# Eight first-product chunks parked in DRAM, two more ahead of the first second product, and top-k casts on ScalarE

## The chip, the cores and the metric

The kernel runs on one core of a Trainium2 chip. The metric is the device time of one execution in microseconds (us), given as the median of several runs. Beside it there is one profiled execution, from which all rows below come. Engines are named as the profile does: PE (TensorE matmul), PEld (its weight loads), DVE (VectorE), ACT (ScalarE), POOL (GpSimd), SP (SyncE, which issues DMAs).

## What is computed

A residual block over 512 tokens of width 1024: a mixer (chunked attention and a state-space layer), a cross-attention, and an expert layer. Only the expert layer is touched. It has 16384 experts of one neuron each, whose keys are pairs out of 128 × 128; each of 8 heads picks 16 experts for a token.

```python
def _peer_ffn(hn, w_q, sub_keys, u_tab, v_tab):
    ...
    def block(xb):                       # 128 tokens
        q = (xb @ w_q).reshape(PEER_BLOCK, PEER_HEADS, 2, PEER_QDIM // 2)
        s = jnp.einsum('thsd,hsnd->thsn', q, sub_keys).astype(jnp.float32)
        sv, si = lax.top_k(s, PEER_TOPK)
        cand = (sv[:, :, 0, :, None] + sv[:, :, 1, None, :]).reshape(PEER_BLOCK, PEER_HEADS, -1)
        cidx = (si[:, :, 0, :, None] * PEER_KEYS + si[:, :, 1, None, :]).reshape(PEER_BLOCK, PEER_HEADS, -1)
        top, pos = lax.top_k(cand, PEER_TOPK)
        e = jnp.take_along_axis(cidx, pos, axis=-1)
        g = jax.nn.softmax(top, axis=-1)
        act = jax.nn.gelu(jnp.einsum('thkd,td->thk', u_tab[e], xb), approximate=False)
        w = (g * act).astype(xb.dtype)
        return jnp.einsum('thk,thkd->td', w, v_tab[e])
```

## The kernel before

The 512 tokens are four blocks of 128. Three of them (384 tokens) are computed densely: all 16384 experts are gone through in 128 chunks of 128, and a table of gates, mostly zeros, picks the chosen ones. The fourth block is gathered: 128 rows of the first table and 128 of the second are fetched for each token by indirect DMAs on POOL's queue, and DVE multiplies and adds them.

The work on the path has four stages.

1. *Top-k* (about 500 to 660 us in the trace). For each head h, `queries(h)` makes the queries and scores on PE, and ACT copies them out of PSUM (`pqT`, `sc`, `scl`). `topk(h, scs, g)` then works for the token blocks of group g (blocks 0 and 1, block 2, block 3): DVE finds the 16 best of each half (`tv`, `ti`), casts their places to float (`tf`), DVE adds the candidates (`ca`) and POOL their numbers (`cx`), DVE finds the 16 best candidates and their places (`pi`, cast to `pf`). A one-hot of the places (`eq`, DVE) times the numbers (`ev`, POOL), summed by DVE (`ex`), gives the experts' numbers. Beside it run 12 chunks of the first product (`FREE`), their splits on POOL.
2. *Gate table* (`build_w`, about 664 to 818 us). 96 half steps: DVE builds one-hots (`oAE`, `oB`), PE multiplies them (eight matmuls `pw` for a half step), ACT copies the results out (two evictions `stg`), and `Wd` in DRAM takes them. 16 chunks of the first product are spread over these half steps (`LEAD - FREE`), six matmuls at a time.
3. *The loop* `for n in range(128)`. `u_phase(n + 28)` is a chunk of the first product: `load_split` fetches 512 KB of the first table, ACT casts them to the rounded type (`whi`), DVE takes the rest (`wlo`); 24 matmuls of 128x384 go to `pa`, and ACT's Gelu writes an activation tile. `v_phase(n)` is a chunk of the second product: the activation times the table of gates `wt` (DVE), rounded (`ah`, ACT), rest (`al`, DVE), and 18 matmuls of 128x512 into the six accumulators `acc`. The gathers are spread over this loop by a rate (`due`). Block 3's top-k, one head an iteration, runs beside iterations 1 to 8.
4. *The end*: the last 28 iterations hold no first product.

There are 31 activation tiles (`LEAD + 3`). The program text is recorded, and the order of each engine's rows is then set by a list scheduler that simulates the times; `tc.issue_after(x)` ties a row behind the row `x`. DMAs are issued by SP (weights, the table's stores) and ACT (the table's loads). Every engine works through its rows in order.

Of the kernel before, what the change touches and what calls it, by code (L numbers as in the profile page):

```python
# [9 lines left out]
F32 = mybir.dt.float32  # L10
# [5 lines left out]
AF = mybir.ActivationFunctionType  # L16
OP = mybir.AluOpType
AX = mybir.AxisListType
# [783 lines left out]
NT = 384  # L802
LEAD = 28
FREE = 12
HOLD = 10
IOH = 2
ULV = (8,)
KS = 2
H0 = 2
SLACK = 4  # L810
# [5 lines left out]
NC_ = sum(n * w for _, n, w in ROWS)  # L816
# [3 lines left out]
def peer(tc, I, c, out):  # L820
# [5 lines left out]
    with tc.tile_pool(name="pp", bufs=1) as pp, tc.tile_pool(name="tq", bufs=2) as tq:  # L826
# [3 lines left out]
        def act_tile(name):  # L830
            return pp.tile([128, NT], F32, tag="act", name=name, bufs=LEAD + 3)
# [45 lines left out]
        def topk(h, scs, g):  # L877
# [11 lines left out]
            tf = tq.tile([128, 2, nb, 16], F32, tag="tf", name="tf")  # L889
            V.tensor_copy(tf, ti)  # L890
            V.tensor_scalar(tf[:, 0], tf[:, 0], 128.0, None, op0=OP.mult)
            ca = tq.tile([128, nb, NC_], F32, tag="ca", name="ca")
# [12 lines left out]
            for b in range(nb):  # L905
# [5 lines left out]
                V.max_index(pi[:, b, 8:16], tb[:, 8:16], cb)  # L911
            V.tensor_copy(pf, pi)
            for b in range(nb):
                sh = [128, NC_, 16]
                eq = tq.tile(sh, BF16, tag="eq", name="eq")
                ev = pp.tile(sh, F32, tag="ev", name="ev", bufs=1)
                V.tensor_tensor(eq, iob, pf[:, b].unsqueeze(1).broadcast_to(sh), op=OP.is_equal)
                G.tensor_tensor(ev, eq, cx[:, b].unsqueeze(2).broadcast_to(sh), op=OP.mult)
                V.tensor_reduce(ex[:, b0 + b, h], ev.rearrange("p n k -> p k n"), axis=AX.X, op=OP.add)  # L919

# [120 lines left out]

        def u_steps(n):
            w = load_split(I["ut"][n], G if n < FREE else V)
            pa = pst("s", "pa")[:, :NT]
            for k in range(8):
                mm3(pa, [t[:, k] for t in w], [PTh(k)[:, 128:], PTl(k)[:, 128:]], k == 0, k == 7)
                if k < 7 and (k + 1) % KS == 0:
                    yield
            acts[n] = act_tile("act")
            S.activation(acts[n], pa, AF.Gelu)  # L1050
            yield

        def u_phase(n):
            for _ in u_steps(n):
                pass
# [3 lines left out]
        def load_wt(i):  # L1059
            wts[i] = wt = s8([128, 12, 128], "wt")  # L1060
            nc.scalar.dma_start(wt, Wd[i].rearrange("i s c t -> i s (c t)"))

        def v_phase(n):
# [13 lines left out]
            if n % 4 == WTP and n + 4 < 128:  # L1077
                with tc.issue_after(c.ah_ins):
                    load_wt(n // 4 + 1)
            c.v_ins = V.tensor_tensor(al, a, ah, op=OP.subtract).ins  # L1080
            for b in range(3):
# [9 lines left out]
        for n in range(FREE):  # L1091
            u_phase(n)
        steps = (None for n in range(FREE, LEAD) for _ in u_steps(n))
        done = 0
        for q in range(96):
            next(gw)
            if q in LATE:
                i = LATE.index(q)
                with tc.issue_after(c.w_ins):
                    gates(1) if i == H0 else topk_late(8 - H0 + i, 1)  # L1100
            with tc.issue_after(c.pw_ins):
                while done < (q + 1) * (8 // KS) * (LEAD - FREE) // 96:
                    next(steps)
                    done += 1
# [4 lines left out]
        for n in range(128):  # L1109
            if n + LEAD < 128:  # L1110
                u_phase(n + LEAD)
            v_phase(n)
# [10 lines left out]
            if n > HOLD:  # L1123
                due += 256 * (2 if n + LEAD < 128 else 1) / (256 - LEAD - 2 * HOLD - SLACK)
            while due >= 1:
# [80 lines left out]
```

## Time and profile before

| what | value |
|---|---|
| median of three runs | 1779.57 us |
| lowest and highest | 1777.91 and 1783.63 us |
| the profiled execution | 1780.63 us, of which the span 1778.9 us |
| PE busy | 1682.0 us of the span |
| DVE, ACT, POOL busy | 1398.8, 717.6, 689.5 us |

The span is the stretch between the first and the last instruction that the profiler records; 1.7 us lie around it. Busy shares are means over stages with different limits, so they are read by stage below. A matmul's own duration is longer than the step from one to the next, because they overlap: prices of PE's work are taken from starts.

### The profile page before, as it was taken

To read this page: it belongs to the slowest core of one execution; us is meant where nothing else is said; L and a number is where in the kernel's file an instruction comes from. 1 tells how busy PE (TensorE), PEld (TensorE's weight loads), DVE (VectorE), ACT (ScalarE), POOL (GpSimd) and SP (SyncE) were. 2 spreads that over 40 slices of the span, in tenths; PEclk is the share of its full clock that TensorE was granted. 3 is DMA by queue.
4 is the path that set the end of the run, shared out by engine and by line. 5 is a ranking of instruction groups with operands and counts; after the bars stand their busy time and mean duration, and the time that the engine had idled before them with its cause. 6 is when DMAs were issued, how large, how long until landed. Compare 5 with 4: busy or idle time off the path is not lost.

```text
span 1778.9 us, 24797 instructions
## 1 busy us (share of the span) xinstructions
PE 1682.0 (95%) x8929; PEld 1462.1 (82%) x8929; DVE 1398.8 (79%) x2755; ACT 717.6 (40%) x1161; POOL 689.5 (39%) x566
## 2 busy tenths in 40 slices
PE   7898999999999668899999999999999999999999
PEld 6676778877788667788888999999999999999887
DVE  7998563644589999995998787777777877777886
ACT  4242573432333227785333333333333333333332
POOL 5432232341466651200345444444343434334451
PEclk9998999999999889999999999999999999999999
DMA  5412323220422226786449998888888888888895
GB/s 189 115 55 89 113 101 142 95 83 15 175 92 81 66 72 208 213 238 225 163 151 352 331 334 303 308 313 303 306 315 293 331 311 318 297 315 300 324 366 212
DMA packets 155820, 383.19 MB, mean 215 GB/s; under 512 B 13993, under 2 KB 70825, under 8 KB 155569
## 3 DMA queue, kind: packets, MB, share of 16 engines
q1 hardware_dynamic: 107504, 212.83, 35.1%
q0 software_dynamic: 36864, 134.23, 21.1%
q10 hardware_dynamic: 11328, 34.54, 5.5%
q8 instruction: 70, 1.15, 0.2%
q14 instruction: 54, 0.43, 0.1%
HBM read 348.72 MB, written 32.51 MB: 214 GB/s over the span
## 4 chain that ended last, share of the span: by engine, by line
PE 71%; DVE 22%; issue 3%; DMA 2%; POOL 1%; ACT 1%; SPq 0%; DVEq 0%; ACTq 0%; POOLq 0%
PE acc L1084 27%; PE pa L124 8%; PE pa L126 8%; PE pa L125 8%; PE pv L124 3%; PE pv L126 3%; PE pv L125 3%; DVE oB L1023 2%; DVE oAE L1019 2%; DVE ex L919 2%; DVE wlo L110 2%; PE pS L684 1%; PE po L694 1%; DVE ca L898 1%; PE pw L1028 1%
## 5 line engine op out<-in xcount | busy, mean ns | idle before, releaser
L108 ACT ACTIVATE whi<-wraw 128x1024 fp32r<-128x1024 f32 (+1 forms) x332 | 349.7, 1055 | 486.9 <-PE pa L125 229.9
L124 PE MATMUL pa<-PTh,whi 128*128 128x384 f32 x1024 | 355.8, 347 | 21.9 <-ACT act L1050 18.2
L126 PE MATMUL pa<-PTh,wlo 128*128 128x384 f32 x1024 | 350.5, 342 | 14.2 <-POOL wlo L110 10.8
L110 DVE TENSOR_TENSOR wlo<-wraw,whi 128x1024 fp32r<-128x1024 f32 x262 | 321.1, 1226 | 53.4 <-ACT whi L108 53.1
L125 PE MATMUL pa<-PTl,whi 128*128 128x384 f32 x1024 | 349.4, 341 | 0.0
L972 POOL DMA_INDIRECT vg<-in_peer_v_dram,ei x128 | 182.1, 1423 | 240.0 <-DVE X L973 216.7
L962 POOL DMA_INDIRECT ug<-in_peer_u_dram,ei x128 | 177.5, 1386 | 225.2 <-DVE ug L963 201.0
L1084 PE MATMUL acc<-wlo,ah 128*128 128x512 f32 x768 | 238.6, 392 | 0.8 <-DVE wlo L110 0.8
L1084 PE MATMUL acc<-whi,ah 128*128 128x512 f32 x768 | 239.2, 392 | 0.0
L1084 PE MATMUL acc<-whi,al 128*128 128x512 f32 x768 | 237.3, 391 | 0.0
L124 PEld LDWEIGHTS pa<-PTh,whi 128*128 128x128 f32 x1024 | 196.6, 192 | 28.1 <-ACT act L1050 20.3
L110 POOL TENSOR_TENSOR wlo<-wraw,whi 128x1024 fp32r<-128x1024 f32 x70 | 170.2, 2441 | 126.7 <-ACT whi L108 126.6
L126 PEld LDWEIGHTS pa<-PTh,wlo 128*128 128x128 f32 x1024 | 196.8, 192 | 17.2 <-POOL wlo L110 12.4
L125 PEld LDWEIGHTS pa<-PTl,whi 128*128 128x128 f32 x1024 | 196.7, 192 | 3.8
L973 DVE SCALAR_TENSOR_TENSOR X<-vg,dots,X 128x1024 f32<-128x1024 f32 x128 | 164.5, 1285 | 16.3 <-DMA vg<-in_peer_v_dram,ei 10.4
L1076 ACT ACTIVATE ah<-act 128x384 fp32r<-128x384 f32 x128 | 67.1, 526 | 260.7 <-PE acc L1084 241.5
L1084 PEld LDWEIGHTS acc<-wlo,ah 128*128 128x128 f32 x768 | 144.6, 188 | 33.3 <-DVE wlo L110 1.5
L1084 PEld LDWEIGHTS acc<-whi,al 128*128 128x128 f32 x768 | 144.1, 188 | 30.9
L963 DVE SCALAR_TENSOR_TENSOR ug<-ug,X 128x1024 f32<-128x1024 f32 x128 | 151.9, 1222 | 20.6 <-DMA ug<-in_peer_u_dram,ei 20.5
L1084 PEld LDWEIGHTS acc<-whi,ah 128*128 128x128 f32 x768 | 143.2, 188 | 23.7
L1080 DVE TENSOR_TENSOR al<-act,ah 128x384 fp32r<-128x384 f32 x128 | 70.9, 555 | 58.7 <-ACT ah L1076 56.3
L1074 DVE TENSOR_TENSOR act<-act,wt 128x384 f32<-128x384 f32 x128 | 66.0, 576 | 58.3 <-DMA wt<-Wd 58.3
(383 smaller groups left out, 2721.9 us busy)
## 6 DMA issues: line engine op xcount, KB each, us to landing
wraw<-in_ut_dram SPq DMA_DIRECT2D x128, 512.0 KB, 5.0
wraw<-in_peer_v_dram SPq DMA_DIRECT2D x128, 512.0 KB, 5.5
Wd<-stg SPq DMA_DIRECT2D x24, 1024.0 KB, 6.5
wt<-Wd ACTq DMA_DIRECT2D x32, 768.0 KB, 7.9
wraw<-in_w_pq_dram SPq DMA_DIRECT2D x16, 512.0 KB, 3.3
h<-in_x_dram SPq DMA_DIRECT2D x8, 512.0 KB, 7.2
wraw<-in_w_qk_dram SPq DMA_DIRECT2D x8, 512.0 KB, 3.7
wraw<-in_w_mk_dram SPq DMA_DIRECT2D x8, 512.0 KB, 3.3
```

What stands on the lines that cost most here:

```text
L108: S.activation(hi, raw, AF.Copy)
L110: ins = leng.tensor_tensor(lo, raw, hi, op=OP.subtract).ins
L124: P.matmul(out, lhs[0], rhs[0], start=first, stop=False)
L125: P.matmul(out, lhs[0], rhs[1], start=False, stop=False)
L126: P.matmul(out, lhs[1], rhs[0], start=False, stop=last)
L962: G.indirect_dma_start(out=ug, out_offset=None, in_=I["peer_u"], in_offset=IOX(ap=ei[:, k:k + 1], axis=0))
L963: V.scalar_tensor_tensor(ug, ug, 1.0, c.X0, op0=OP.mult, op1=OP.mult, accum_out=dots[:, k:k + 1])
L972: G.indirect_dma_start(out=vg, out_offset=None, in_=I["peer_v"], in_offset=IOX(ap=ei[:, k:k + 1], axis=0))
L973: V.scalar_tensor_tensor(a0, vg, dots[:, k:k + 1], a0, op0=OP.mult, op1=OP.add)
L1076: c.ah_ins = S.activation(ah, a, AF.Copy).ins
L1080: c.v_ins = V.tensor_tensor(al, a, ah, op=OP.subtract).ins
L1084: P.matmul(acc[b * 2 + d], l[:, b * 128:(b + 1) * 128], v[r][:, d * 512:(d + 1) * 512], start=n == 0 and l is ah and r == 0, stop=n == 127 ...
```

## The change

It has four parts.

- Casts: the places `ti` and `pi` are cast by ACT in place of DVE. The scaling by 128 of the first half goes into the cast, so a head has three ACT instructions where it had three DVE instructions.
- Layout: `ev` is laid out by place first, 16 x 54 in place of 54 x 16. DVE's sum reads it contiguously, and POOL's product writes it at a step of 54 values (216 bytes).
- Eight more chunks ahead: the first product's order is chunks 120 to 127 first, then 0 to 119 (`UORDER`). The first eight activation tiles are stored to DRAM (`Ad`) by ACT's queue right behind their Gelu, and their buffers are free again. They are loaded back at iterations 117 to 124, three before their use. So 36 chunks stand ahead of the loop with the same number of tiles, 24 of them spread over the gate table.
- Two more (`AHEAD`) are written between the table and the first second product. The last 38 iterations hold no first product, and the rate of gathers is set anew, from 512/204 to 512/194 for an iteration with a first product.

```diff
 LEAD = 28
+NSPILL = 8
+AHEAD = 2
...
-            V.tensor_copy(tf, ti)
-            V.tensor_scalar(tf[:, 0], tf[:, 0], 128.0, None, op0=OP.mult)
+            S.activation(tf[:, 0], ti[:, 0], AF.Copy, scale=128.0)
+            S.activation(tf[:, 1], ti[:, 1], AF.Copy)
...
-            V.tensor_copy(pf, pi)
+            S.activation(pf, pi, AF.Copy)
...
-                ev = pp.tile(sh, F32, tag="ev", name="ev", bufs=1)
+                ev = pp.tile([128, 16, NC_], F32, tag="ev", name="ev", bufs=1)
...
-                G.tensor_tensor(ev, eq, cx[:, b].unsqueeze(2).broadcast_to(sh), op=OP.mult)
-                V.tensor_reduce(ex[:, b0 + b, h], ev.rearrange("p n k -> p k n"), axis=AX.X, op=OP.add)
+                G.tensor_tensor(ev.rearrange("p k n -> p n k"), eq, cx[:, b].unsqueeze(2).broadcast_to(sh), op=OP.mult)
+                V.tensor_reduce(ex[:, b0 + b, h], ev, axis=AX.X, op=OP.add)
...
-        def u_steps(n):
-            w = load_split(I["ut"][n], G if n < FREE else V)
+        UORDER = [*range(128 - NSPILL, 128), *range(128 - NSPILL)]
+        Ad = c.dr.tile([NSPILL, 128, NT], F32, name="Ad")
+
+        def u_steps(j):
+            n = UORDER[j]
+            w = load_split(I["ut"][n], G if j < FREE else V)
...
-            acts[n] = act_tile("act")
-            S.activation(acts[n], pa, AF.Gelu)
+            a = act_tile("act")
+            S.activation(a, pa, AF.Gelu)
+            if j < NSPILL:
+                nc.scalar.dma_start(Ad[j], a)
+            else:
+                acts[n] = a
...
+            if 0 <= n + 3 - (128 - NSPILL) < NSPILL:
+                with tc.issue_after(c.ah_ins):
+                    acts[n + 3] = act_tile("act")
+                    nc.scalar.dma_start(acts[n + 3], Ad[n + 3 - (128 - NSPILL)])
...
-        steps = (None for n in range(FREE, LEAD) for _ in u_steps(n))
+        steps = (None for n in range(FREE, LEAD + NSPILL) for _ in u_steps(n))
...
-                while done < (q + 1) * (8 // KS) * (LEAD - FREE) // 96:
+                while done < (q + 1) * (8 // KS) * (LEAD + NSPILL - FREE) // 96:
...
-            if n + LEAD < 128:
-                u_phase(n + LEAD)
+            if n == 0:
+                for j in range(AHEAD):
+                    u_phase(LEAD + NSPILL + j)
+            if n + LEAD + NSPILL + AHEAD < 128:
+                u_phase(n + LEAD + NSPILL + AHEAD)
...
-                due += 256 * (2 if n + LEAD < 128 else 1) / (256 - LEAD - 2 * HOLD - SLACK)
+                due += 256 * (2 if n + LEAD + NSPILL + AHEAD < 128 else 1) / (256 - LEAD - NSPILL - AHEAD - 2 * HOLD - SLACK)
```

The first place is the end of the gate table and the stretch up to the first second product, in ACT's rows, because each chunk has one Gelu (`act<-pa`) there and each half step two evictions (`stg<-pw`). Before:

```order
L1031 ACTIVATE stg<-pw 128x4x64 x12
L108 ACTIVATE whi<-wraw 128x1024
L1050 ACTIVATE act<-pa 128x384
L1031 ACTIVATE stg<-pw 128x4x64 x12
L108 ACTIVATE whi<-wraw 128x1024
L1050 ACTIVATE act<-pa 128x384
L108 ACTIVATE whi<-wraw 128x1024
L1050 ACTIVATE act<-pa 128x384
L1061 DMA wt<-Wd 128x1536
L108 ACTIVATE whi<-wraw 128x1024
L1050 ACTIVATE act<-pa 128x384
L108 ACTIVATE whi<-wraw 128x1024
```

After, up to the first roundings `ah` and the second load of the table:

```order
L1033 ACTIVATE stg<-pw 128x4x64 x8
L108 ACTIVATE whi<-wraw 128x1024
L1057 ACTIVATE act<-pa 128x384
L1033 ACTIVATE stg<-pw 128x4x64 x8
L108 ACTIVATE whi<-wraw 128x1024
L1057 ACTIVATE act<-pa 128x384
L1072 DMA wt<-Wd 128x1536
L1057 ACTIVATE act<-pa 128x384
L108 ACTIVATE whi<-wraw 128x1024 x2
L1057 ACTIVATE act<-pa 128x384
L1087 ACTIVATE ah<-act 128x384 x2
L1072 DMA wt<-Wd 128x1536
```

A Gelu stood to 12 evictions and now stands to 8, and the table's first load `wt<-Wd` stood behind two Gelu after the last eviction and now stands behind one. In PE's rows (too many to show) 62 first-product matmuls stand between the last `pw` and the first `acc` before, 94 after; from the last `pw` to the end of the program there are 2388 before and 2214 after.

The second place is the late top-k of block 3 in the loop, in DVE's rows: the places `pi`, their cast `pf`, and the one-hots `eq`. Before:

```order
L912 CAST pf<-pi 128x16
L911 MAX_INDEX pi<-top,ca 128x8
L885 MAX_INDEX ti<-tv,sc_8518 128x8 x2
L898 TENSOR_TENSOR ca<-tv 128x8
L898 TENSOR_TENSOR ca<-tv 128x10
L898 TENSOR_TENSOR ca<-tv 128x12
L885 MAX_INDEX ti<-tv,sc_8518 128x8
L110 TENSOR_TENSOR wlo<-wraw,whi 128x1024
L917 TENSOR_TENSOR eq<-iob,pf 128x864
L912 CAST pf<-pi 128x16
```

After:

```order
L913 MAX_INDEX pi<-top,ca 128x8
L912 MAX top<-ca 128x8
L921 TENSOR_REDUCE ex<-ev 128x16
L913 MAX_INDEX pi<-top,ca 128x8
L1095 TENSOR_TENSOR al<-act,ah 128x384
L919 TENSOR_TENSOR eq<-iob,pf 128x864
L110 TENSOR_TENSOR wlo<-wraw,whi 128x1024
L919 TENSOR_TENSOR eq<-iob,pf 128x864
```

The casts are gone from DVE's row, and an `eq` now stands one to four rows behind the `pi` that ACT casts for it.

The third place is ACT's row beside it, in the same iterations. Before, it holds the loop's own work alone:

```order
L1061 DMA wt<-Wd 128x1536
L108 ACTIVATE whi<-wraw 128x1024 x2
L1050 ACTIVATE act<-pa 128x384
L1076 ACTIVATE ah<-act 128x384
L108 ACTIVATE whi<-wraw 128x1024 x2
```

After:

```order
L893 ACTIVATE tf<-ti 128x16
L892 ACTIVATE tf<-ti 128x16
L893 ACTIVATE tf<-ti 128x16
L1087 ACTIVATE ah<-act 128x384
L108 ACTIVATE whi<-wraw 128x1024
L914 ACTIVATE pf<-pi 128x16 x2
L108 ACTIVATE whi<-wraw 128x1024
L1057 ACTIVATE act<-pa 128x384
L1087 ACTIVATE ah<-act 128x384
```

The casts stand between the weight casts, the Gelu and the roundings.

## Rows read from the trace of the kernel before

**Rows 1.** The page, first part: busy time, share and instructions of each engine.

```profile
PE 1682.0 (95%) x8929; PEld 1462.1 (82%) x8929; DVE 1398.8 (79%) x2755; ACT 717.6 (40%) x1161; POOL 689.5 (39%) x566
```

**Rows 2.** Busy by stretch: length; PE, PEld, DVE, ACT, POOL; granted clock, DMA share, GB/s.

```profile
500.00:600.00 100.00, 93.00 (x478) 79.55 (x476) 98.20 (x494) 33.07 (x73) 62.92 (x76) 1.00 0.23 76
600.00:650.00 50.00, 28.25 (x127) 26.97 (x127) 48.38 (x158) 11.49 (x15) 36.11 (x35) 0.76 0.23 75
650.00:800.00 150.00, 129.63 (x1099) 116.43 (x1099) 149.69 (x245) 109.60 (x203) 23.61 (x15) 0.93 0.68 202
...
820.00:850.00 30.00, 26.00 (x122) 22.96 (x123) 20.95 (x79) 9.09 (x15) 0.85 (x5) 0.94 0.64 220
...
900.00:950.00 50.00, 45.41 (x217) 39.95 (x216) 43.98 (x101) 16.72 (x23) 25.31 (x25) 0.97 0.62 215
...
1100.00:1250.00 150.00, 150.00 (x760) 136.51 (x759) 114.01 (x167) 54.50 (x76) 63.15 (x46) 1.00 0.88 307
...
1720.00:1740.00 20.00, 20.00 (x89) 16.54 (x89) 15.31 (x20) 7.66 (x10) 8.73 (x6) 1.00 0.99 381
```

**Rows 3.** The chain that ended last, from 1640 us on: start, length, what.

```profile
1643.77 0.17 PE pa L124
...
1647.95 4.12 PE acc L1084 x18
...
1656.26 118.15 PE acc L1084 x521
```

**Rows 4.** The same chain from 800 to 960 us.

```profile
801.23 0.93 PE pw L1028 x16
...
817.86 0.65 ACT stg L1031
818.53 5.61 DMA Wd<-stg
824.24 6.20 DMA wt<-Wd
...
833.23 4.39 PE acc L1084 x12
...
927.88 6.40 DMA ug<-in_peer_u_dram,ei
```

**Rows 5.** Waits: engine, line, waited for; us in total, times, longest.

```profile
ACT ah L1076 <- PE acc L1084: 241.5, 104, 2.8
```

**Rows 6.** Single lines: shortest, median, longest in ns; first and last start in us.

```profile
L1028 PE MATMUL pw<-oB,oAE x768: 217/218/330, 666.2 to 817.6; 128*128 128x128 f16 x192
...
L890 DVE CAST tf<-ti x24: 151/175/2389, 499.6 to 914.6; 128x32 f32<-128x32 uint32 x16, 128x64 f32<-128x64 uint32 x8
...
L912 DVE CAST pf<-pi x24: 149/182/1648, 501.5 to 918.1; 128x16 bf16<-128x16 uint32 x16, 128x32 bf16<-128x32 uint32 x8
```

**Rows 7.** Groups by line (the two last by shape too): busy us, mean ns of one; idle before.

```profile
L110 DVE TENSOR_TENSOR wlo<-wraw,whi 128x1024 fp32r<-128x1024 f32 x262 | 321.1, 1226 | 53.4 <-ACT whi L108 53.1
...
L918 POOL TENSOR_TENSOR ev<-eq,cx 128x864 f32<-128x864 bf16 x32 | 66.1, 2064 | 100.7 <-DVE eq L917 45.0 <-DVE ex L919 31.4 <-DVE tf L890 15.0
...
L919 DVE TENSOR_REDUCE ex<-ev 128x16 f32<-128x864 f32 x32 | 52.7, 1648 | 3.1 <-POOL ev L918 3.1
...
L912 DVE CAST pf<-pi 128x16 bf16<-128x16 uint32 (+1 forms) x24 | 11.8, 490 | 0.1
...
L870 ACT ACTIVATE scl<-ppS 128x128 f32<-128x128 f32 x32 | 7.1, 280 | 0.0
...
L890 DVE CAST tf<-ti 128x32 f32<-128x32 uint32 (+1 forms) x24 | 6.0, 268 | 0.0
L891 DVE TENSOR_SCALAR tf<-tf 128x16 f32<-128x16 f32 (+1 forms) x24 | 5.8, 254 | 0.0
...
L928 DVE TENSOR_REDUCE gs<-top 128x8 f32<-128x128 f32 x2 | 0.6, 308 | 0.0
...
L928 DVE TENSOR_REDUCE gs<-top 128x16 f32<-128x256 f32 x1 | 0.4, 415 | 0.0
```

## The prediction

> **What bounds the kernel now.** The page's busy shares come first [rows 1]: PE, the engine of the matmuls, is busy 95% of the span, so time comes off only where PE idles or is held at its lower clock. The table by stage says where [rows 2]. In 500–650 (the top-k stage) PE idles 7.0 us in the first 100 us and 21.75 of the last 50, there at a mean granted clock of 0.76, while DVE is busy 98.20 of 100 and 48.38 of 50: DVE and what it feeds set this stage. In 650–800 (the gate table) PE idles 20.4 us of 150 and DVE 0.3: DVE is the bound. In 820–850 PE idles 4.0, in 900–950 4.6. In 1100–1250, which stands for 950–1700, PE is busy all 150 us and DVE 114: here only the number of matmuls counts.
>
> The chain that ends last, near its end, gives the two prices of PE in that steady part [rows 3]: a first-product chunk starts at 1643.77 and the second product behind it at 1647.95, so 4.18 us for 24 matmuls (0.174 each); the second product's 18 take 4.12 us. From 1656.26 on there are only second products, 118.15 us long, to 1774.4.
>
> The same chain between the gate table and the first second product [rows 4]: the last table matmul ends at about 817.86; then one eviction, 5.61 us for the table's store, 6.20 us for its first load, and the first second product starts at 833.23, 15.4 us after the table's last matmul. Later, a wait of 6.40 us for a gather stands in the chain at 927.88.
>
> The waits [rows 5] show how loosely ACT runs in the loop: it waits 241.5 us for PE before the rounding of an activation tile, in 104 waits: 2.3 us on average, 2.8 at most.
>
> **The change part by part.** *Eight more chunks inside the gate table.* In the two orders of PE's rows, 2388 first-product matmuls stand behind the last table matmul before, 2214 after: 174 fewer, at 0.174 us **−30.3 us**. This part is the surest: all of that stretch but the places above is PE at 100%.
>
> They must be paid in the table's stage. The order of ACT shows one chunk to 8 evictions in place of 12, four half steps in place of six. A half step costs PE eight table matmuls, 0.47 us by [rows 4] (16 in 0.93), and now six of the chunk's, 1.05: 1.52 us, where the stage runs at 1.58 (666.2 to 817.6 over 96 half steps [rows 6]). So PE's own work just fits and would alone cost nothing. DVE is full [rows 2], so each chunk's split is paid there: 8 × 1.22 = 9.8 us [rows 7]. Two late top-k heads stand in this stage too, and what the casts and the reduction give back (1.7 us a head, below) makes that +6.4. Bounds: +3 if half of the splits find DVE waiting once it shares its time with a fuller PE; 8 × 4.18 = +33 if PE pays the chunks in full, because the two wait for each other. I take **+9**, near the lower end, since PE's 20 us of idle time and its low clock there (0.93) show that it has room, and a little above DVE's bill for their waits on each other. The eight stores of 192 KB go out on ACT's queue, and what stands behind them there is the next weight cast; ACT is busy 109.6 of 150, and eight chunks more (8 × 1.5 for cast and Gelu) make it 122, which leaves room for eight issues.
>
> *Two more chunks ahead of the first second product.* Before, 62 first-product matmuls stand between the table and the first second product, after, 94. At 0.174 the 62 take 10.8 us of the 15.4, so PE idles 4.6; the 94 take 16.4 and fill it: **−4.6 us**. Bounds 0 and −4.6: the two extra 512 KB loads run beside the table's store and load, and may delay these. In the order of ACT the load of the table, whose issue waits for the store, now stands ahead of a Gelu; the chunk behind it can still be written to the other of the two PSUM buffers.
>
> *Casts on ACT, the contiguous reduction.* A DVE reduction of 864 values read at a stride takes 1.65 us [rows 7]. The contiguous ones in the kernel take 308 ns for 128 values and 415 for 256, 0.84 ns a value, which for 864 gives 0.92 us: 0.6 to 0.7 less each, and I take 0.65. The three casting operations of a head take 0.49 + 0.27 + 0.25 = 1.01 us by their means [rows 7], but these hold runs that stood blocked: two medians are 175 and 182 ns, the longest 2389 and 1648 [rows 6]; at 0.18 for each of the three it is 0.54. The top-k stage has 8 heads of two token blocks and 6 of one, so 14 heads and 22 reductions: 14.1 + 14.3 = 28 us by means, 7.6 + 14.3 = 22 by medians. A late head, of one block, gives 1.01 + 0.65 = 1.7. The Trainium skill, "SBUF — State Buffer", section "SBUF: two separate sides", says that DVE operations which use the second port, and GpSimd operations, hold one port pair in turn and block each other for a whole instruction; by this the blocked time is not saved but falls on the next such DVE operation, and the relief would be the 22. The rows agree with it so far (a cast of 175 ns that once took 2389), but no run here has shown where the time goes.
>
> DVE is not alone in this stage: POOL is busy 36 of 50 in 600–650, and the matmuls of the queries wait for casts on ACT. PE's idle time in 500–650 is 28.75 us and cannot all go. I take half of the relief, **−14 us**; bounds 0 and −25. What is late next is POOL's product, which the reduction waits for, and the Gelu tiles.
>
> On ACT each cast costs at most what its 128-value copies do, 0.28 us [rows 7], 72 of them some 20 us over the kernel, in stages where it is busy under half of the time but in the gate table's. In order, though, a cast that waits for DVE holds what stands behind it. In the loop the order shows such a cast of the candidates' places between a weight cast and the rounding of an activation tile; the equality on DVE that needs it stands one to four rows behind its source. The slack named above (2.3 us a wait on average) covers a wait of that size, and DVE is relieved of 8 × 1.7 = 13.6 us in 840–950; PE idles 4.6 us in 900–950: **−3**, bounds 0 and −4.6.
>
> *POOL's product, written at a step of 216 bytes.* No row shows such a write on POOL. Nothing changes if a write costs the same at any step: 2.06 us [rows 7]. The nearest row at a long step is the reduction, 1.65 against 0.92, a factor 1.8: 3.7 us. I take 2.06, because it is the two-input arithmetic of this engine that is slow (2.4 ns a value), and an access hides under it; 3.7 is a rival.
>
> *The end.* Eight activation tiles come back from memory, 197 KB each, at iterations 117 to 124, 1.6 MB in 33 us, on top of a stretch with a DMA share of 0.99 at 381 GB/s [rows 2]; ten iterations more run without a first product, at a slightly higher rate of gathers. The loads alone at 381 GB/s take 4.1 us, and half can hide: **+2**, bounds 0 and +6.
>
> Sum: −30.3 + 9 − 4.6 − 14 − 3 + 2 = −40.9. The profiled execution took 1780.63 for a span of 1778.9, which gives 1739.7; it was 1.06 above the median of the three runs, so **1739 us**.
>
> **The rivals.** *The table's stage pays in full.* For it: DVE and PE are both above 85% there, and waits of one feed the other; against it: 20 us of idle PE. +33 for +9 gives 1763.
> *POOL's strided write costs 3.7 us.* 22 of them in the top-k stage at 1.6 more are 36 us on an engine that has 63 busy in 500–600 and 36 of the next 50: the gain of the stage goes, 1739 + 14 = 1753. The Trainium skill, "SBUF — State Buffer", section "Specifications (TRN2)", has lines of 16 bytes and asks for two hits on each for full bandwidth; the reduction's row agrees, and by that rule the change only moves the cost from a reader to a writer. Both of these together give 1777, within what can't be told from no change.
> *The end is short of DMA, and the two chunks ahead gain nothing.* +6 for +2 and 0 for −4.6: 1748.
> *Slower: ACT in order in the loop.* Each of eight late heads puts three casts in ACT's row, and each waits for DVE, which itself waits for ACT's weight casts behind. If the three cost 2.8 us each of the loop, the largest such wait in [rows 5], it is 8 × 8.4 = 67 us less the 13.6 of relief: +53 in place of −3, 1795. It decides from about 6.4 us a head on ((40.9 + 13.6 − 3) / 8). For it: the casts stand close behind what they wait for; against it: ACT's slack, and DVE's order lets other work pass between.
> *The change doesn't do what it says:* the orders show that it does, and the parts stand in this text by their order.
>
> **How the numbers follow.** The forecast 0.60; the table in full 0.13; POOL's write 0.10; both 0.05; the end 0.05; ACT in order 0.07. A difference under 0.3%, 5.3 us, can hardly be told from no change here. Faster: 0.60 + 0.13 + 0.10 + 0.05 = 0.88; same 0.05; slower 0.07. The range takes in the bounds of the top-k stage below (−25 for −14: 1728, and with +3 for the table 1722) and the table's rival above: 1721 to 1764.
>
> **What would show it.** In the profile after: 2214 first-product matmuls behind the table; the table's stage 3 to 15 us longer with DVE still full; PE without a gap between the last table matmul and the first second product; the reduction at 0.9 to 1.1 us; the product on POOL at about 2.1; the top-k stage 10 to 20 us shorter; second products from about 1577 on without a gap, to the end. It would be wrong if the table's stage grew by over 20 us, if the product took over 3 us, or if PE's row in the first ten iterations held waits for casts on ACT.

## The result, and the profile after

The changed kernel takes 1738.75 us (median of four runs, 1737.47 to 1739.86), the kernel before 1779.52: a ratio of 0.9767, 95% interval 0.9749 to 0.9785. The forecast was 1739. The profiled execution took 1737.47 for a span of 1735.7, so span against span the change is −43.2 us where the sum said −40.9; the median of the changed kernel lies 1.3 us above its profiled execution, that of before lay 1.1 below, which closes the gap by chance.

The table by stage of the changed kernel, with the columns of [rows 2]:

```profile
500.00:600.00 100.00, 93.62 (x465) 80.56 (x463) 96.41 (x519) 36.69 (x104) 73.86 (x82) 0.97 0.25 82
600.00:650.00 50.00, 39.48 (x205) 38.25 (x206) 45.28 (x100) 17.95 (x30) 30.99 (x28) 0.90 0.33 114
650.00:800.00 150.00, 143.05 (x1228) 127.69 (x1227) 141.82 (x228) 122.78 (x227) 27.91 (x12) 0.98 0.75 224
...
820.00:850.00 30.00, 30.00 (x157) 27.77 (x156) 22.41 (x69) 13.51 (x23) 2.75 (x6) 1.00 0.74 243
850.00:900.00 50.00, 50.00 (x255) 45.54 (x254) 46.59 (x167) 18.47 (x37) 21.94 (x30) 1.00 0.45 144
900.00:950.00 50.00, 47.26 (x233) 42.62 (x232) 42.65 (x105) 19.66 (x31) 23.82 (x26) 0.97 0.75 259
...
1100.00:1250.00 150.00, 150.00 (x759) 136.51 (x759) 115.37 (x170) 54.26 (x76) 69.31 (x49) 1.00 0.89 313
```

Three things are to be seen. PE idles 10.5 us in 600–650 where it idled 21.75, and at a granted clock of 0.90 for 0.76. In 820–850 it does not idle at all. And in 650–800 the roles have changed: DVE, which had 0.3 us to spare, now has 8.2, and PE, which idled 20.4 us, idles 7.0: the gate table has gone from DVE's stage to PE's.

Two single lines mark the stages, with the columns of [rows 6]: the table's matmuls and the second products, by the starts of the first and the last.

```profile
L1030 PE MATMUL pw<-oB,oAE x768: 217/218/330, 649.0 to 814.6; 128*128 128x128 f16 x192
```

```profile
L1099 PE MATMUL acc<-whi,ah x768: 389/389/632, 831.0 to 1730.2; 128*128 128x512 f32 x192
```

The first table matmul comes at 649.0 for 666.2 (−17.2 us), the table takes 165.6 for 151.4 (+14.2). Of the 17.2, 1.5 lie ahead of the top-k stage, where nothing was changed: its first `tv` comes at 487.9 for 489.4. From the last table matmul to the last second product it was 955.7 us (817.6 to 1773.3) and is 915.6 (814.6 to 1730.2): −40.1. Together −43.1.

The chain that ended last shows PE's own pace in the table, one group of eight table matmuls and six of a chunk, and the end:

```profile
811.16 0.48 PE pw L1030 x8
...
812.75 0.48 PE pw L1030 x8
...
814.33 0.48 PE pw L1030 x8
...
831.18 4.12 PE acc L1099 x18
```

```profile
1572.30 158.95 PE acc L1099 x701
```

A half step takes 1.585 us when only PE is in the way. The last stretch has 701 second-product matmuls in 158.95 us, 0.2267 each; before it was 521 in 118.15 [rows 3], 0.2268 each. So nothing is lost at the end.

The waits of PE between 500 and 960 us, with the columns of [rows 5], of the kernel after, and below them the three largest of before:

```profile
PE pa L124 <- ACT act L1057: 10.1, 3, 3.7
PE wtp L992 <- DVE f L989: 10.0, 2, 5.4
PE acc L1099 <- DVE wlo L110: 2.7, 1, 2.7
```

```profile
PE pa L124 <- ACT act L1050: 18.2, 6, 12.6
PE pw L1028 <- DVE oB L1023: 17.2, 19, 2.7
PE pa L126 <- POOL wlo L110: 10.8, 4, 7.4
```

The wait of the table's matmuls for DVE (17.2 us) has all but gone (1.4). One wait has grown: the transposes `wtp`, by which the lists of a token block are prepared for the table, wait for DVE's small operations `f`, 10.0 us in place of 3.4; one of the two waits, 5.4 us, lies inside the table, the other ahead of it.

The new forms of the moved operations, shortest, median and longest (DVE's reduction, POOL's product, ACT's cast), and POOL's product before:

```profile
L921 DVE TENSOR_REDUCE ex<-ev x32: 1024/1040/1055, 503.2 to 919.0; 128x16 f32<-128x864 f32 x32
```

```profile
L920 POOL TENSOR_TENSOR ev<-eq,cx x32: 1776/2090/6288, 501.0 to 915.7; 128x864 f32<-128x864 bf16 x32
```

```profile
L914 ACT ACTIVATE pf<-pi x24: 198/216/235, 499.9 to 911.6; 128x16 bf16<-128x16 uint32 x16, 128x32 bf16<-128x32 uint32 x8
```

```profile
L918 POOL TENSOR_TENSOR ev<-eq,cx x32: 1655/1902/6347, 502.6 to 922.1; 128x864 f32<-128x864 bf16 x32
```

### The profile page after: what moved, and what is told of

It is laid out like the page before. It is cut to its first block, busy times and chain, and to the rows that moved or that the text cites. A ratio compares the mean times of both kernels' runs of the same rounds, so it can differ in the third digit from the quotient of the medians.

```text
span 1735.7 us, 24863 instructions
## 1 busy us (share of the span) xinstructions
PE 1670.3 (96%) x8929; PEld 1450.5 (84%) x8929; DVE 1363.3 (79%) x2683; ACT 732.0 (42%) x1233; POOL 719.6 (41%) x566
## 4 chain that ended last, share of the span: by engine, by line
PE 72%; DVE 20%; issue 2%; POOL 2%; DMA 2%; ACT 1%; SPq 0%; DVEq 0%; ACTq 0%; POOLq 0%
PE acc L1099 28%; PE pa L124 8%; PE pa L125 8%; PE pa L126 8%; PE pv L124 3%; PE pv L126 3%; PE pv L125 3%; DVE wlo L110 2%; PE pw L1030 2%; POOL ev L920 1%; PE pS L684 1%; DVE oB L1025 1%; DVE ca L900 1%; DVE ex L921 1%; DVE oAE L1021 1%
## 5 line engine op out<-in xcount | busy, mean ns | idle before, releaser
L124 PE MATMUL pa<-PTh,whi 128*128 128x384 f32 x1024 | 354.7, 346 | 10.2 <-ACT act L1057 10.1
L126 PE MATMUL pa<-PTh,wlo 128*128 128x384 f32 x1024 | 346.7, 339 | 0.0
L974 POOL DMA_INDIRECT vg<-in_peer_v_dram,ei x128 | 192.1, 1500 | 211.3 <-DVE X L975 184.3
L964 POOL DMA_INDIRECT ug<-in_peer_u_dram,ei x128 | 186.1, 1454 | 201.5 <-DVE ug L965 176.6
L900 POOL TENSOR_TENSOR cx<-tf 128x8 f32<-128x8 f32 (+6 forms) x120 | 43.0, 393 | 188.7 <-ACT tf L893 188.5
L1033 ACT ACTIVATE stg<-pw 128x256 f32<-128x256 f32 x192 | 103.8, 683 | 26.0 <-PE pw L1030 20.4
```

Source lines behind the costliest of these rows:

```text
L124: P.matmul(out, lhs[0], rhs[0], start=first, stop=False)
L126: P.matmul(out, lhs[1], rhs[0], start=False, stop=last)
L964: G.indirect_dma_start(out=ug, out_offset=None, in_=I["peer_u"], in_offset=IOX(ap=ei[:, k:k + 1], axis=0))
L974: G.indirect_dma_start(out=vg, out_offset=None, in_=I["peer_v"], in_offset=IOX(ap=ei[:, k:k + 1], axis=0))
L1033: S.activation(stg[e][:, :, q * 8 + hf * 4:q * 8 + hf * 4 + 4].rearrange("p i t -> p t i"), pw.rearrange("p (t i) -> p t i", t=4)[:, :, e ...
```

## The experiments

All kernels are read by the same six numbers. The *top-k stage* runs from the first `tv`, DVE's first search for the 16 best, to the first table matmul. The next columns come from the two lines shown above (starts of the table's matmuls and of the second products), and from the orders of PE's rows (first-product matmuls behind the table). *Waits behind the table* is worked out: from the last table matmul to the last second product, less PE's own work there at the prices of [rows 3], which is 0.1742 us for each first-product matmul and 526.3 us for the second products (128 × 4.12, less 1.1 because the last one is taken at its start).

| kernel | median, us | top-k stage | first table matmul | table | behind it, of that matmuls | waits behind the table |
|---|---|---|---|---|---|---|
| before | 1779.5 | 176.8 | 666.2 | 151.4 | 955.7, 2388 | 13.4 |
| changed | 1738.75 | 161.1 | 649.0 | 165.6 | 915.6, 2214 | 3.6 |
| topk_only | 1753.0 | 160.7 | 648.0 | 147.2 | 948.6, 2406 | 3.2 |
| chunks_only | 1761.2 | 175.7 | 664.1 | 169.0 | 920.8, 2214 | 8.8 |
| casts_back | 1747.0 | 172.5 | 660.3 | 161.4 | 916.6, 2214 | 4.6 |
| ev_back | 1748.6 | 165.6 | 654.3 | 168.4 | 918.7, 2214 | 6.7 |
| prep_split | 1734.1 | 161.5 | 653.6 | 159.4 | 915.9, 2214 | 3.9 |
| splits_pool | 1739.0 | 161.4 | 652.2 | 166.3 | 915.6, 2214 | 3.6 |
| no_ahead | 1736.7 | 161.6 | 650.3 | 166.0 | 912.8, 2214 | 0.8 |
| spill4 | 1742.1 | 160.7 | 646.7 | 151.1 | 934.6, 2310 | 5.9 |
| ahead_only | 1776.85 | 177.2 | 665.9 | 149.9 | 952.9, 2388 | 10.6 |
| restore2 | 1749.2 | 161.4 | 649.3 | 165.9 | 929.2, 2214 | 17.2 |
| ev_contig | 1748.3 | 174.8 | 663.4 | 165.0 | 914.9, 2214 | 2.9 |
| split_no_ahead | 1732.8 | 161.2 | 652.4 | 160.1 | 913.3, 2214 | 1.3 |

Each row comes from one profiled execution, and executions of one kernel lie up to 8.5 us apart. Much of that lies ahead of the top-k stage, in work that no edit touches: the first `tv` starts anywhere from 486.0 to 492.1 us, and moves the first table matmul with it. The stages themselves repeat better: the top-k stage is 160.7 to 161.6 us long in the eight kernels that hold both top-k edits as in the changed kernel, 175.7 to 177.2 in the three that hold neither. In two kernels the order differs by one chunk: in `casts_back` and `ev_contig` 288 first-product matmuls stand ahead of the table and 570 inside it, where the changed kernel has 264 and 594. These 24 matmuls, 4.2 us, lengthen the top-k stage there and shorten the table.

**The two halves: `topk_only` and `chunks_only`.** The first is the kernel before with only the casts and the layout; the second leaves these out (by the two edits that stand below under `casts_back` and `ev_back`) and keeps the chunks.

```diff
-NSPILL = 8
-AHEAD = 2
```

> The kernel before with the casts on ACT and the contiguous reduction, and nothing of the chunks. Theory (the parts add up): in the changed kernel the table's first matmul came 17.2 us earlier (649.0 for 666.2), and the stalls of the loop shrank by about 5; these belong to the top-k edits alone, and two late heads give the table 2 to 3 us back. So 1779.5 - 17 - 5 - 2 = 1755, between 1752 and 1760, with the table's first matmul at about 649. Rival (the top-k stage gained because the chunks moved): the first matmul stays above 660, time 1768 or more.

> The changed kernel with the casts back on DVE and the old layout of the product: only the eight parked chunks and the two ahead are left. Theory: 30.3 us less matmul work behind the table and 4.6 us of PE's wait filled, against a table that is 14 to 17 us longer (14.2 measured, and up to 3 us that the casts no longer give back): 1779.5 - 30.3 - 4.6 + 16 = 1761, between 1757 and 1766. Rival (without the relief DVE makes the table pay in full, +33): 1778.

Measured: `topk_only` 1753.02 (ratio 0.9855, interval 0.9836 to 0.9874), `chunks_only` 1761.23 (0.9902, 0.9883 to 0.9922). Both are where the theory put them, and both rivals fall. The top-k edits alone shorten the top-k stage by 16.1 us and take 10 us out of the waits behind the table; the chunks alone leave the top-k stage nearly as it was (175.7). Added, the two gains are 26.5 + 18.3 = 44.8 us against 40.8 measured together. By the profiles some 5 us of waits behind the table can only be taken away once (10.2 and 4.6 alone, 9.8 together); the medians alone, of four runs each, would not show a difference of this size.

**Which of the top-k edits: `casts_back` and `ev_back`.**

```diff
-            S.activation(pf, pi, AF.Copy)
+            V.tensor_copy(pf, pi)
```

```diff
-                ev = pp.tile([128, 16, NC_], F32, tag="ev", name="ev", bufs=1)
+                ev = pp.tile(sh, F32, tag="ev", name="ev", bufs=1)
```

(In the first, the cast of `tf` goes back too; in the second, the product and the reduction go back to the old layout.)

> The changed kernel with the casts back on DVE. Theory (casts relieve DVE, in part only): by medians 14 heads x 0.54 us = 7.6 us of DVE in the top-k stage and 4.3 in the loop, half of it on the path: +4 to +8, 1743 to 1747, and the table's first matmul 3 to 6 us later than 649.0. Rival (blocked time only moves on to the next operation, and POOL's product sets the stage): within 2 us of 1738.7.

> The changed kernel with the old layout of the product (the reduction reads at a step again). Theory: 32 reductions at 1.65 in place of 1.04 us are 19.5 us of DVE, 13.4 of them in the top-k stage; POOL's product falls from a median of 2.09 to 1.90 us. The larger half of the top-k gain: +8 to +12, 1747 to 1751, the first table matmul 6 to 10 us later than 649.0. Rival (POOL's product sets the stage, and a contiguous write makes it faster): 1739 or less.

Measured: 1747.02 (0.982, 0.9803 to 0.9837) and 1748.64 (0.983, 0.9812 to 0.9847). Each edit is worth 8 to 10 us, and the rivals, by which one of them does nothing, fall. Up to the end of the table the two weigh the same. Without the casts the top-k stage is 11.4 us longer and the table 4.2 shorter; the chunk that this order moved ahead of the table is 4.2 of both, so 7.2 us are the casts' (3 to 6 were expected). Without the layout the stage is 4.5 us longer and the table 2.8, together 7.3 (6 to 10 expected for the stage alone). Behind the table the waits are 3.1 us longer without the layout and 1.0 without the casts. PE's waits from 500 to 700 us in `casts_back` show one thing that the casts did in the stage:

```profile
PE pa L124 <- ACT act L1057: 15.1, 4, 9.7
PE pa L126 <- POOL wlo L110: 5.5, 1, 5.5
```

A first-product chunk waits for ACT's Gelu 9.7 us at once; before it was 12.6, in the changed kernel 3.7 at most, in `ev_back` 3.8. With the casts on DVE that Gelu stands behind the exponential of the first gates in ACT's row, and the exponential waits for DVE: 12.6 us before and 9.3 in `casts_back` (first line). In `ev_back` (second line) it starts as late and waits for nothing, since ACT has by then waited in pieces, 7.4, 5.1 and 3.3 us, before the casts in its row.

```profile
623.29 0.42 ACT L929 ACTIVATE top<-top 128x256 f32<-128x256 f32 x1 [9.31 <-DVE top L928]
```

```profile
623.05 0.42 ACT L929 ACTIVATE top<-top 128x256 f32<-128x256 f32 x1
```

So the one long wait goes mainly because the casts stand in ACT's row and split it. That DVE is further on is the smaller part: the operation that the exponential reads ends at 621.5 us in `ev_back` and at 623.3 in `casts_back`.

**Who sets the table's pace: `prep_split` and `splits_pool`.** The first writes the four small DVE operations of the third block's preparation earlier, and its transposes later (by the edit they are eight half steps apart, not the six of its expectation). The second gives POOL the splits of eight of the 24 chunks in the table.

```diff
-                    if (b, sb) == PREP:
-                        prepare(2)
...
+                        if (b, sb, q) == (1, 2, 2):
+                            f2 = pre(2)
+                        if (b, sb, q) == (1, 3, 2):
+                            prepare(2, f2)
```

```diff
-            w = load_split(I["ut"][n], G if j < FREE else V)
+            w = load_split(I["ut"][n], G if j < FREE or FREE <= j < LEAD + NSPILL and j % 3 == 0 else V)
```

> The changed kernel with the preparation of the table's third block cut in two: its four small DVE operations are written six half steps earlier than its transposes, and the transposes four half steps later than before. Theory (in the table's stage PE stood 5.4 us before a transpose for DVE's small operations, and ran at the lower clock behind it): the table takes 158 to 161 us in place of 165.6, time 1731 to 1735. Rival (DVE sets the table's pace and the wait is only the place where its lag shows): the table keeps its 165 us, time within 2 us of 1738.7.

> The changed kernel with the splits of eight of the 24 chunks in the table's stage (every third) on POOL in place of DVE: DVE is spared 8 x 1.22 = 9.8 us, as if the eight more chunks cost it nothing. Theory (PE's own pace, 1.585 us a half step, and its wait before the transpose set the table): at most 4 us, 1734 to 1740. Rival (the DVE bill of my sum): the table 9 to 10 us shorter, 1729.

`prep_split` took 1734.09 (0.9735, 0.9708 to 0.9762): the table is 159.4 us long, 6.2 less, and of the two long waits before transposes only the one ahead of the table is left (the second fence: what ended the transposes' waits, us, times). The time's interval overlaps that of the changed kernel (0.9749 to 0.9785), so the gain is read from the table.

```profile
L1037 PE MATMUL pw<-oB,oAE x768: 217/218/238, 653.6 to 813.0; 128*128 128x128 f16 x192
```

```profile
  DVE f L989: 4.7, 1
```

`splits_pool` took 1738.98 (0.9768, 0.9745 to 0.979), with a table of 166.3 us, not one shorter. But it did not relieve DVE, and so does not test the bill. DVE has 19 splits in the table for 26, and yet is busy 158.1 us of it, where it was 150.5. Beside each of POOL's seven splits in the table one of DVE's one-hot operations took 2.3 to 3.2 us, in place of the usual 0.68 (`oB`) or 1.2 (`oAE`). The line of `oB`, in the changed kernel and here, and one such pair:

```profile
L1025 DVE TENSOR_TENSOR oB<-oAE,gp x96: 668/684/695, 646.2 to 806.2; 128x1024 f16<-128x1024 f16 x96
```

```profile
L1025 DVE TENSOR_TENSOR oB<-oAE,gp x96: 666/679/2833, 651.3 to 810.2; 128x1024 f16<-128x1024 f16 x96
```

```profile
721.28 2.65 POOL L110 TENSOR_TENSOR wlo<-wraw,whi 128x1024 fp32r<-128x1024 f32 x1 [0.49 <-ACT whi L108]
```

```profile
721.65 3.43 DVE L1025 TENSOR_TENSOR oB<-oAE,gp 128x1024 f16<-128x1024 f16 x2
```

POOL's split ends at 723.93, and the first of the two `oB` 0.56 us behind it. PE's wait before the transpose is gone in this run too, and other waits for DVE's one-hots stand in its place (5.1 us in the table for 1.4). So what these two runs show is that PE's wait before the transpose is 6 us of the table; what DVE's bill is worth there has to come from the next run.

**The price of a chunk: `spill4`.**

```diff
-NSPILL = 8
+NSPILL = 4
```

> The changed kernel with four parked chunks in place of eight. 4 x 4.18 = 16.7 us of matmuls go back behind the table. Theory (the table is paid in part): it gets 6 to 10 us shorter than 165.6, time 1738.7 + 16.7 - 8 = 1747, between 1745 and 1750. Rival (each chunk is paid in full in the table): it gets 16 us shorter, 1739. Rival (the table's length is DVE's, 1.22 us a chunk): 5 us shorter, 1751.

Measured: 1742.10 (0.9796, 0.9775 to 0.9817), the table 151.1 us.

```profile
L1030 PE MATMUL pw<-oB,oAE x768: 217/218/330, 646.7 to 797.8; 128*128 128x128 f16 x192
```

That is none of the three as written, and nearest to the one that I had not held: the table gets 14.5 us shorter, close to the 16 of "paid in full" and nearly three times the 5 of DVE's bill. Set beside `topk_only`, which has none of the eight (147.2), the price is not one price: the first four chunks cost the table 3.9 us, 1.0 each, and the next four 14.5, 3.6 each, of the 4.18 that they save behind it. With the transposes out of the way (`prep_split`) the last four still cost 8.3, 2.1 each. PE's own work says where the kink comes from. At 0.48 us for a group of eight table matmuls and 0.1742 for each first-product matmul (402, 498 and 594 stand in the table in the traces) it is an estimated 116, 133 and 150 us, which leaves PE 31 us to spare in `topk_only`, 18 in `spill4` and 16 in the changed kernel. The first four chunks went into that room, the next four hardly found any. Why 16 to 18 us of it cannot be filled is shown only for the 6 of the preparation.

**The two chunks ahead: `no_ahead` and `ahead_only`.** They are taken out of the changed kernel, and put alone into the kernel before.

```diff
-AHEAD = 2
+AHEAD = 0
```

> The changed kernel without the two chunks ahead of the first second product. Theory: the 15.4 us that the table's store and load take are filled by fewer first-product matmuls, and 4 to 6 us of PE's wait come back: 1743 to 1745, with the table as long as in the changed kernel. Rival (the two extra loads delay the table's load by as much as they fill): 1739.

> The kernel before with only the two chunks ahead of the first second product: 86 first-product matmuls stand in that stretch in place of 62. Theory (my sum): they fill 4.2 of the 4.6 us that PE idles there, 1775.5. Rival (as taking them out of the changed kernel gave no loss: the work only changes its place, since a chunk less stands in a later iteration where PE then waits): 1779 to 1781.

`no_ahead` took 1736.66 (0.9754, 0.973 to 0.9779): no loss that the runs can show, where I had 4 to 6. In its order 78 first-product matmuls stand between the table and the first second product without any being put there, where before had 62. They fill 13.6 us of a stretch that is now 14.0 long (816.3 to 830.3).

```profile
L1099 PE MATMUL acc<-whi,ah x768: 389/389/496, 830.3 to 1729.1; 128*128 128x512 f32 x192
```

`ahead_only` took 1776.85 (0.9985, 0.9975 to 0.9995): 2.5 us gained of the 4.2, between the theory and the rival. Its stages show where the rest went:

```profile
840.00:850.00 10.00, 10.00 (x52) 9.02 (x51) 8.30 (x27) 4.48 (x6) 4.60 (x6) 1.00 0.57 181
850.00:900.00 50.00, 48.30 (x244) 43.52 (x242) 48.44 (x185) 15.97 (x22) 16.67 (x30) 1.00 0.41 139
900.00:950.00 50.00, 43.78 (x211) 38.93 (x212) 44.80 (x112) 17.77 (x25) 23.25 (x24) 0.97 0.68 225
```

The stretch up to 850 is full, but PE now idles 7.9 us in 850–950, where it had idled 4.6, all of it in 900–950 [rows 2]: the wait is partly passed on to the late top-k.

**The end: `restore2`.** Each parked tile is loaded back twice.

```diff
+                    nc.scalar.dma_start(acts[n + 3], Ad[n + 3 - (128 - NSPILL)])
```

> The changed kernel with each of the eight parked tiles loaded back twice, 1.6 MB more in the last iterations. Theory (from the trace of the changed kernel: the last 158.95 us hold second products without a gap, so the loads are hidden): within 2 us of 1738.7. Rival (my sum's +2 for the end: the stretch is at its DMA bound): +4, the loads' full time at 381 GB/s, 1743.

Measured: 1749.21 (0.9823, 0.9803 to 0.9843), over twice what either had. The chain of this kernel says why:

```profile
1674.88 3.64 PE acc L1100 x16
...
1678.60 0.35 ACT ah L1087
...
1678.99 20.30 DMA act<-Ad
...
1699.31 0.33 ACTq L1095
```

The second load writes the tile of the first, so its issue on ACT's queue waits until the first has landed, 20.30 us after its issue; the residual's and the table's loads were issued on the same queue just before it. ACT stands there, with the weight casts behind. So this run does not tell what 1.6 MB more would cost; it shows how long such a load takes in this stretch, and what a wait on ACT's queue costs. The price of the extra traffic alone stays open.

**POOL's write: `ev_contig`.** The one-hot is laid out by place first too (the numbers `iob` that it is compared with go along), so that POOL's product reads and writes contiguously.

```diff
-                V.tensor_tensor(eq, iob, pf[:, b].unsqueeze(1).broadcast_to(sh), op=OP.is_equal)
-                G.tensor_tensor(ev.rearrange("p k n -> p n k"), eq, cx[:, b].unsqueeze(2).broadcast_to(sh), op=OP.mult)
+                V.tensor_tensor(eq, iob, pf[:, b].unsqueeze(2).broadcast_to(sh), op=OP.is_equal)
+                G.tensor_tensor(ev, eq, cx[:, b].unsqueeze(1).broadcast_to(sh), op=OP.mult)
```

> The changed kernel with the one-hot laid out by place first too, so that POOL reads and writes contiguously and DVE's equality broadcasts the place along its inner axis. Theory (the write at a step costs POOL 0.1 to 0.2 us, the shortest product was 1.78 for 1.66 us): the product is back at a median of 1.90, the equality gets no faster; 1736 to 1739. Rival (a long step costs as at the reduction, and what hides it is only the lock): the product well under 1.6 us, 1730.

Measured: 1748.34 (0.9819, 0.9802 to 0.9837), slower than the changed kernel. The product and the equality here, and the equality of the changed kernel:

```profile
L920 POOL TENSOR_TENSOR ev<-eq,cx x32: 1769/2460/6125, 502.2 to 934.4; 128x864 f32<-128x864 bf16 x32
```

```profile
L919 DVE TENSOR_TENSOR eq<-iob,pf x32: 1031/1046/2633, 501.0 to 932.2; 128x864 bf16<-128x864 bf16 x32
```

```profile
L919 DVE TENSOR_TENSOR eq<-iob,pf x32: 583/602/2457, 500.3 to 913.9; 128x864 bf16<-128x864 bf16 x32
```

The product's shortest time is 1.77 us here and 1.78 in the changed kernel, but that does not make the step free. This edit changes two things for POOL, the write and the way it reads `cx`: 54 values in a row, where each value was repeated 16 times. The kernels that differ in the write alone say more. With the old layout (before, `chunks_only`, `ev_back`, `ahead_only`) the shortest product takes 1.66 us and the median is 1.90 to 1.96; with the step (the changed kernel and the seven others with both edits) 1.76 to 1.78 and 2.06 to 2.09; `casts_back`, with the step too, lies higher (1.86 and 2.12). So the step costs POOL 0.1 to 0.2 us, as the theory had, and the rival of a product well under 1.6 us falls. The equality went from a median of 602 ns to 1046. The top-k stage is 13.7 us longer, 4.2 of it the chunk that stands ahead of the table in this order; why the product's median rose to 2.46 is not settled.

**The two gains together: `split_no_ahead`.** `prep_split` with `AHEAD = 0`.

> The changed kernel with the preparation of the third block cut in two, and without the two chunks ahead of the first second product: the two edits that gained by themselves, 4.7 and 2.1 us. Theory (they act at different places): 1732, between 1729 and 1735. Rival (the 2.1 was scatter): 1734 to 1736.

Measured: 1732.76 (five runs, 1730.42 to 1733.14; 0.9725, 0.9711 to 0.9738). Its interval lies below that of the changed kernel, so the two edits together beat it. That they beat `prep_split` alone is not shown (0.9725 and 0.9735, with intervals that overlap), so the rival, by which the 2.1 was scatter, stays open.

## Why the prediction was right, point by point

*The matmuls behind the table.* 2214 for 2388, −30.3 us: right. The stretch behind the table shrank by 40.1, and the 9.8 above that are waits (13.4 to 3.6).

*The waits behind the table.* I had −4.6 for the stretch before the first second product, −3 for the late top-k and +2 for the end, −5.6 in all; it was −9.8. The step that failed is **"the 94 take 16.4 and fill it: −4.6"**, in what it was credited to. PE is indeed busy in all of that stretch (16.4 us for 94 matmuls), but `no_ahead` fills it with 78 and loses nothing. The two chunks ahead are worth nothing that the runs can show in the changed kernel, and 2.5 us alone. The casts and the layout do most of it: alone they bring the waits from 13.4 to 3.2, and DVE is spared 10.5 us in its late heads behind the table (18.8 us of casts and reductions before, 8.3 after), where the sum had 13.6. The term for them was too small, since I had counted only the idle time of 900–950.

*The table.* **"I take +9"** was too small: +14.2. I priced the chunks by DVE's splits because DVE was the busy engine before. After the change the stage passes to PE. Its pace is 1.585 us a half step (152 us in all), where the sum had 1.52 and let it cost nothing; a wait for the third block's preparation comes on top (6.2 us by `prep_split`), and some 7 us over the rest, 3.1 of them 18 first-product matmuls beyond six a half step (594 for 576). The other 4 no run took away. The rival "the table pays in full" was wrong for the first four chunks (1.0 us each) and nearly right for the next four (3.6 each).

*The top-k stage.* −14, it was −15.7 from the first `tv` on (176.8 to 161.1). "Half of the relief" of 28 us was a choice, and it was near. By `casts_back` and `ev_back` the casts and the layout are worth 7.2 and 7.3 us up to the end of the table, each about half, as the sum had given them. The reduction was at 1.04 us, inside the 0.9 to 1.1 expected. The Trainium skill, "SBUF — State Buffer", section "SBUF: two separate sides", says that DVE operations with two inputs in SBUF and POOL operations that read it take one port pair in turn, and that the later one is fully blocked. The trace of `splits_pool` agrees: an `oB` that began beside a POOL split ended 0.56 us behind it, a little under its usual length of 0.68. The prediction drew from this section that the casts could give back no more than their 7.6 us by medians; 7.2 do not contradict it, and no run here separates it from other causes.

*POOL's write at a step.* "I take 2.06": the median was 2.09, but 1.90 with the old layout, so the step costs 0.1 to 0.2 us where the sum had put nothing. The prediction had taken the mean of before, 2.06, which holds a few long runs (6.35 us the longest). The rival of 3.7 us fell. The Trainium skill, "SBUF — State Buffer", section "Specifications (TRN2)", states a penalty for each access that goes to a new line of 16 bytes. DVE's reduction agrees (1.65 us at a step of 64 bytes, 1.04 contiguous); POOL's product pays at most a tenth, so the cost did not move from the reader to the writer, as the prediction's rival had it.

*ACT in order.* The casts waited 40.2 us for the places `pi` (16 times) and 51.3 for the places `ti` (22 times), but in the loop PE is busy all 50 us of 850–900 and waits once, 2.7 us, for a split on DVE: the rival by which the change would be slower has no trace there. The slack that [rows 5] showed was there. In the top-k stage the mechanism does show, though small: two of PE's three waits for the Gelu, 3.7 and 3.2 us, end behind a cast for which ACT had stood 7.1 and 2.7 us.

*The end.* +2 was a bound's half; by the chain it is 0. The sentence that put the eight stores into the table's stage was wrong: the parked chunks are the first eight, and their stores were issued from 592.7 to 630.5, in the top-k stage, where nothing waited for them.

So the sum held because a table that cost 5 us more met waits that gave 4 us more, a top-k stage that gave 2 us more and 1.5 us of scatter ahead of it. The surest term and most of the signs were right; that the median fell within 1 us of the forecast is luck.

## What to carry to other kernels

The price of work moved into a stage is that of the engine which bounds the stage after the move, and it has a kink: ask how much fits under the present bound (here four chunks at 1.0 us each), and price what is beyond by the next engine (3.6 us each, 1.5 of it a wait that could be moved away). Before a run is taken to show that an engine's work does not matter, its busy time must have fallen: in `splits_pool` it rose. And before two starts are compared, subtract what lies ahead of the change, and count the matmuls ahead of each. Where two edits fill the same gap, taking each out of the final kernel says more than adding each to the first one. A small operation that is spread along a full engine's row, like the preparation here, should be written well ahead of what waits for it.

## What the hardware showed unexpectedly

An equality of 864 bf16 values on DVE took 602 ns with one operand repeated along the outer axis and 1046 ns with it repeated along the inner one. POOL's product of the same size took 1.78 us at best with a write at a step of 216 bytes and 1.66 without, while DVE's reduction gained a factor 1.6 from reading contiguously. Eight splits moved from DVE to POOL made DVE busier, by 7.5 us in the table, because its one-hot operations stood beside them for up to 3.2 us. And a load of 192 KB issued on ACT's queue took 20.30 us to land in a stretch where the DMA share was 1.02 (`restore2`).
